# Token-major copies in an RWKV-7 mixer: tensor-engine transposes in place of products with the identity

## The chip, the cores and the metric

The kernel runs on one core of a Trainium2 chip. The metric is the device time of one execution in microseconds, the median of several runs. The engines are TensorE (PE for its matmuls, PEld for its weight loads), VectorE (DVE), ScalarE (ACT), GpSimd (POOL) and SyncE (SP). SyncE, ScalarE and GpSimd also issue DMA transfers.

## The reference

A decoder trunk of two layers runs one step for a prompt (1 sequence of 256 tokens) and a group of samples (8 sequences of 8 tokens), all in float32, with width 1024. Each layer is half a SwiGLU FFN, a token mixer, and half a SwiGLU FFN, each with RMSNorm and a shift, scale and gate that come from a conditioning vector ("ada" below). Layer 0 mixes with a Griffin recurrent block, layer 1 with RWKV-7. The change lies in RWKV-7, which runs this recurrence for 16 heads of 64:

```python
def wkv_scan(r, w, k, v, a, b, S0):
    def step(S, inp):
        r_t, w_t, k_t, v_t, a_t, b_t = inp
        sa = jnp.einsum('bhvk,bhk->bhv', S, a_t)
        S = S * w_t[:, :, None, :] + sa[..., None] * b_t[:, :, None, :] + v_t[..., None] * k_t[:, :, None, :]
        return S, jnp.einsum('bhvk,bhk->bhv', S, r_t)
```

The outputs are the new activations and all recurrent states.

## The kernel before

Prompt and samples are laid side by side as T = 320 columns (256 prompt tokens, then 64 sample tokens). Activations are kept feature-major: a tile is 128 partitions of features by tokens, and there are NT = 8 such tiles, each with two heads. Weights are streamed from HBM by `Weights`: SyncE loads a block of 512 KB into one of five `raw` buffers, and for the large products ScalarE (line 80) and VectorE (line 82) split it into a high and a low part in float32r. `mm3` (lines 174 to 176) then multiplies with three matmuls per block: high by high, high by low, low by high. The conditioning rows come from `Ada` (`ada_ps`, line 190); its `finish` turns them feature-major with transposes of the tensor engine (`ada_tr`, line 206).

RWKV-7 is computed in chunks of 64 tokens: four of the prompt and one of the samples (C5 = 5). A chunk needs copies of some operands with tokens on the partitions. The kernel makes them on TensorE: the feature-major data is the stationary operand, the 128 by 128 identity `eye` streams past it, and the result in PSUM is copied to SBUF. Three places do so:

- `prep(i)`, once per tile: `zw` and `za` (decay and rate), norms `pn` (line 869), `pb` (line 875), the chunk products `g` (line 885), which `mask` turns into the small triangular matrices in `MP` (prompt) and `MS` (samples), and at its end `dt` (line 904): for each of the 5 chunks a 128 by 128 transposed copy of `kk`, evicted by ScalarE into `Dt` (line 905). The bank is PSUM bank 6 for both pieces (chunks 0 to 3, then chunk 4).
- `v_tok(i)`, once per tile: `vt` (line 1078), the values of each chunk in token-major form. The 64 tokens of a chunk go to partitions 64 to 127 of the output, and ScalarE evicts them into the lower half of `UV` (line 1079). Chunks 0 to 3 use bank 2, chunk 4 bank 6.
- `x0t(p)`, four times: `xt` (line 1037), eight 64 by 32 blocks of the inverse `X` each, evicted into `X0T` by ScalarE, and in the call p = 0 by ScalarE and VectorE (lines 1039 and 1040). All are in bank 2.

Between them lies a triangular solve. `prep` sends its small matrices to DRAM (`Mp`, `Ms`) and `invert_s` and `invert_p` load the diagonal blocks back. VectorE inverts the 8 by 8 blocks of the samples and, in 31 steps `s` (lines 976 and 978), the 32 by 32 blocks of the prompt. While it does, TensorE projects the values (`vproj_all`, step V), makes `vt` (step T), multiplies `pw` in `w0` (step O, line 1116; its output is on partitions 0 to 63), and works on the last ada block (step A). Then follow `xt` (step X), the write of `X` to DRAM and the copies of its blocks back into `MP` and `XD` (step D, lines 1046 to 1056), the two products `z` and `x01` of `double` (step Z, lines 1092 and 1101), the samples (`smp`, steps a0 to a7, lines 1133 to 1175), and the chunk recurrence (steps C).

The order of all that is a list written out by hand, `MID`, in which each name takes the next step of its thread:

```python
p7 p7 I V V V V I V V s s s s s s s s V T s s s s s s s s s s A A T s T s s T s T A T A O O s s A s s O A O A
T A s s T s O X X O O A a0 s s X a1 a0 a0 a1 O A A D a0 a0 a2 a2 a2 a1 a2 a1 a1 a2 X Z L Z Q C C C C C C C G0
```

It is the order in which the program is written; the framework then schedules each engine's instructions by their dependencies and priorities (the ada steps have high priority), so the order on an engine can differ from it.

Of the kernel before, what the change touches and what calls it, by code (L numbers as in the profile page):

```python
# [19 lines left out]
T = TP + NB * TS  # L20
# [100 lines left out]
def trunk_kernel(ctx: ExitStack, tc: tile.TileContext, I: dict, O: dict):  # L121
    nc = tc.nc
# [10 lines left out]
    X = [big.tile([128, NT, T], F32, tag="x", name="x")]  # L133
# [5 lines left out]
    eye = const.tile([128, 128], F32, name="eye")  # L139
# [9 lines left out]
    def bank(n, shape, name):  # L149
        return psum.tile(shape, F32, tag=f"p{n}", name=name)  # L150
# [519 lines left out]
    def rwkv_items(nxt):  # L670
# [3 lines left out]
        R = {}  # L674
# [135 lines left out]
        def prep(w, i):  # L810
# [22 lines left out]
            kk = tp.tile([128, C5, 2, 64], F32, tag="kk", bufs=1, name="kk")  # L833
# [15 lines left out]
            t = tp.tile([128, T], F32, tag="xm", bufs=4, name="tk")  # L849
# [10 lines left out]
            for h in range(2):  # L860
                s = slice(64 * h, 64 * h + 64)
# [38 lines left out]
            for n, (c0, c1) in enumerate(((0, 4), (4, 5))):  # L900
                yield
                dt = bank(6, [128, 4, 128], "dt")
                for c in range(c0, c1):
                    nc.tensor.matmul(dt[:, c - c0], kk[:, c].rearrange("p e t -> p (e t)"), eye, start=True, stop=True)
                nc.scalar.copy(out=Dt[:, c0:c1], in_=dt[:, 0:c1 - c0])

        def k_outer(w, i):
# [52 lines left out]
        for i in range(NT):  # L960
            step("R", lambda w, i=i: proj_rk(w, 0, i), [(I["rkv"][0, i], True, 1024)])
            step("v", lambda w, i=i: part_v(w, i))
            steps(f"p{i}", 8, lambda w, i=i: prep(w, i), [(I["w2a2"][i], False, 128)])
# [66 lines left out]
        def x0t(w, p):  # L1030

            if p == 3:
                R["X0T"] = big.tile([32, 64, 32], F32, tag="x", name="X0T")
            X = R["solve"][1]
            ps = bank(2, [32, 8, 64], "xt")
            for s in range(8):
                nc.tensor.matmul(ps[:, s], X[0:64, 8 * p + s], eye[0:64, 0:64], start=True, stop=True)
            o = R["X0T"][:, :, 8 * p:8 * p + 8].rearrange("t m s -> t s m")
            nc.scalar.copy(out=o[:, 0:4], in_=ps[:, 0:4])
            (nc.scalar.copy if p else nc.vector.tensor_copy)(out=o[:, 4:8], in_=ps[:, 4:8])  # L1040
# [28 lines left out]
        def v_tok(w, i):  # L1069
            if i == 0:  # L1070
                R["UV"] = [big.tile([128, 4, C5, 2, 64], F32, tag=n, name="UV") for n in ("xh", "xl")]
            vv = R["v"][:, i]
            nc.gpsimd.memset(R["UV"][i // 4][0:64, i % 4], 0.0)
            uv = R["UV"][i // 4][64:128, i % 4]
            for n, (c0, c1) in enumerate(((0, 4), (4, 5))):
                vt = bank((2, 6)[n], [128, 4, 128], "vt")
                for c in range(c0, c1):
                    nc.tensor.matmul(vt[64:128, c - c0], vv[:, c * 64:c * 64 + 64], eye, start=True, stop=True)
                nc.scalar.copy(out=uv[:, c0:c1].rearrange("p c h v -> p c (h v)"), in_=vt[64:128, 0:c1 - c0])
            nc.vector.tensor_tensor(out=R["bv"][:, i], in0=R["bv"][:, i], in1=vv, op=ALU.mult)  # L1080

        for i in range(NT):
            step("V", lambda w, i=i: vproj_all(w, i), [(I["rkv"][2, i], True, 1024)])
            step("T", lambda w, i=i: v_tok(w, i))
# [96 lines left out]
        for p in (3, 2, 1, 0):  # L1181
            step("X", lambda w, p=p: x0t(w, p))
# [405 lines left out]
```

## Time and profile before

| | |
|---|---|
| median of 3 runs | 1481.87 us (1481.76 to 1485.55) |
| profiled execution | 1483.55 us |
| its span, first to last instruction | 1481.7 us |
| mean granted TensorE clock | 0.987 |
| TensorE busy | 1434.0 us, 97% |
| VectorE, ScalarE, GpSimd busy | 865.1, 670.8, 63.7 us |
| DMA traffic | 266.58 MB, mean 180 GB/s |

All times in views of the profile are counted from the first instruction. A matmul's recorded duration includes its way through the array, so consecutive matmuls overlap in the record, and the distance between their starts is what each costs when they follow each other. The page's chain of work follows the end of the program back from releaser to releaser. In rows by line, "x" is the number of instructions.

### The profile page before, as it was taken

Reading aid. Unit: us, or ns where it says so; the run is one execution under the profiler, and the core shown is the slowest. Engines: PE = TensorE matmul, PEld = TensorE weight load, DVE = VectorE, ACT = ScalarE, POOL = GpSimd, SP = SyncE. Lnnn points to the kernel's source line nnn. Section 1 sums busy time; section 2 is a strip of 40 time slices with the busy share of each in tenths; the row PEclk is TensorE's granted clock in tenths of the full one; section 3 lists DMA queues with packets and bytes.
Section 4 is the critical chain, followed back from the end, with each engine's and each line's share of the span. In section 5 each row is a group of like instructions: output and inputs, shape, how many; then the busy total and the mean of one; then the engine's idle time right before and its main releaser. Section 6 shows DMA issues by size and latency. Waiting matters only on the chain.

```text
span 1481.7 us, 25886 instructions
## 1 busy us (share of the span) xinstructions
PE 1434.0 (97%) x10436; PEld 1307.8 (88%) x10436; DVE 865.1 (58%) x1674; ACT 670.8 (45%) x1215; POOL 63.7 (4%) x170
## 2 busy tenths in 40 slices
PE   5999999999999999999999999999998999999997
PEld 1999999989889999998999998688956779999997
DVE  6644445598874445557444446787754589444444
ACT  4433333488553333445333434386536446343431
POOL 0000000031000000000000003000022100000000
PEclk9999999999999999999999999999999999999998
DMA  8785745457366674546645555223564143444442
GB/s 344 297 302 214 279 139 154 153 207 274 135 238 245 227 269 134 151 149 229 231 176 213 177 152 171 98 70 94 153 218 140 64 154 128 155 157 143 145 148 70
DMA packets 92537, 266.58 MB, mean 180 GB/s; under 512 B 25024, under 2 KB 27456, under 8 KB 91904
## 3 DMA queue, kind: packets, MB, share of 16 engines
q1 hardware_dynamic: 83344, 256.31, 49.9%
q10 hardware_dynamic: 8976, 8.35, 1.8%
q8 instruction: 82, 1.34, 0.4%
q0 software_dynamic: 96, 0.26, 0.1%
q14 instruction: 39, 0.32, 0.1%
HBM read 257.86 MB, written 7.03 MB: 179 GB/s over the span
## 4 chain that ended last, share of the span: by engine, by line
PE 90%; DVE 5%; ACT 2%; DMA 1%; issue 1%; POOL 0%; DVEq 0%; ACTq 0%; POOLq 0%
PE po L176 8%; PE po L174 8%; PE po L175 8%; PE pu L174 7%; PE pg L174 7%; PE pg L176 7%; PE pg L175 7%; PE pu L175 7%; PE pu L176 7%; PE ada_ps L190 5%; PE g L885 1%; PE ps_p L176 1%; PE ps_p L174 1%; PE ps_p L175 1%; DVE lo L82 1%; PE ps_l L769 1%
## 5 line engine op out<-in xcount | busy, mean ns | idle before, releaser
L80 ACT CAST hi<-raw 128x1024 fp32r<-128x1024 f32 (+1 forms) x333 | 340.7, 1023 | 600.7 <-issue 247.9
L82 DVE TENSOR_TENSOR lo<-raw,hi 128x1024 fp32r<-128x1024 f32 (+1 forms) x333 | 396.4, 1191 | 324.9 <-ACT hi L80 324.0
L174 PE MATMUL po<-hh,hi 128*128 128x320 f32 x704 | 217.5, 309 | 0.0
L175 PE MATMUL po<-hl,hi 128*128 128x320 f32 x704 | 217.5, 309 | 0.0
L176 PE MATMUL po<-hh,lo 128*128 128x320 f32 x704 | 217.5, 309 | 0.0
L174 PE MATMUL pu<-mh,hi 128*128 128x320 f32 x608 | 189.9, 312 | 1.5 <-ACT hi L80 1.5
L174 PE MATMUL pg<-mh,hi 128*128 128x320 f32 x608 | 188.5, 310 | 0.0
L176 PE MATMUL pg<-mh,lo 128*128 128x320 f32 x608 | 187.9, 309 | 0.0
L176 PE MATMUL pu<-mh,lo 128*128 128x320 f32 x608 | 187.8, 309 | 0.0
L175 PE MATMUL pg<-ml,hi 128*128 128x320 f32 x608 | 187.8, 309 | 0.0
L175 PE MATMUL pu<-ml,hi 128*128 128x320 f32 x608 | 187.8, 309 | 0.0
L174 PEld LDWEIGHTS po<-hh,hi 128*128 128x128 f32 x704 | 132.1, 188 | 0.0
L175 PEld LDWEIGHTS po<-hl,hi 128*128 128x128 f32 x704 | 132.1, 188 | 0.0
L176 PEld LDWEIGHTS po<-hh,lo 128*128 128x128 f32 x704 | 132.1, 188 | 0.0
L174 PEld LDWEIGHTS pu<-mh,hi 128*128 128x128 f32 x608 | 114.1, 188 | 12.9 <-ACT g L425 10.9
L174 PEld LDWEIGHTS pg<-mh,hi 128*128 128x128 f32 x608 | 114.1, 188 | 5.0 <-ACT hh L418 3.4
L175 PEld LDWEIGHTS pu<-ml,hi 128*128 128x128 f32 x608 | 114.2, 188 | 0.0
L176 PEld LDWEIGHTS pg<-mh,lo 128*128 128x128 f32 x608 | 114.1, 188 | 0.0
L176 PEld LDWEIGHTS pu<-mh,lo 128*128 128x128 f32 x608 | 114.1, 188 | 0.0
L175 PEld LDWEIGHTS pg<-ml,hi 128*128 128x128 f32 x608 | 114.1, 188 | 0.0
L431 DVE TENSOR_TENSOR u<-pu,g 128x320 f32<-128x320 f32 x76 | 37.4, 492 | 127.8 <-PE pu L176 127.8
L190 PE MATMUL ada_ps<-ada_w,sct 128*32 128x512 f32 x448 | 55.0, 610 | 0.0
(383 smaller groups left out, 2405.0 us busy)
## 6 DMA issues: line engine op xcount, KB each, us to landing
raw<-in_ffn_in SPq DMA_DIRECT2D x176, 512.0 KB, 3.2
ada_w<-in_ada_w SPq DMA_DIRECT2D x28, 2048.0 KB, 8.5
raw<-in_ffn_out SPq DMA_DIRECT2D x64, 512.0 KB, 3.5
raw<-in_ada_w SPq DMA_DIRECT2D x32, 512.0 KB, 5.0
raw<-in_ffn_out SPq DMA_DIRECT2D x32, 384.0 KB, 3.1
raw<-in_rkv SPq DMA_DIRECT2D x18, 512.0 KB, 3.2
raw<-in_lru_in SPq DMA_DIRECT2D x16, 512.0 KB, 3.7
raw<-in_lru_out SPq DMA_DIRECT2D x8, 512.0 KB, 3.2
```

Of the source, the lines that this page charges most:

```text
L80: self.nc.scalar.copy(out=hi[:, :n], in_=raw[:, :n])
L82: self.nc.vector.tensor_tensor(out=lo[:, :n], in0=raw[:, :n], in1=hi.bitcast(F32)[:, :n], op=ALU.subtract)
L174: nc.tensor.matmul(ps[:, :n], a, xh[:, k0 + k, :n], start=st, stop=False)
L175: nc.tensor.matmul(ps[:, :n], a, xl[:, k0 + k, :n], start=False, stop=False)
L176: nc.tensor.matmul(ps[:, :n], b, xh[:, k0 + k, :n], start=False, stop=sp)
L190: mm = nc.tensor.matmul(self.ps[r:r + 32, :], sct[:, k, :], wh[:, q * 512:q * 512 + 512], start=(k == 0), stop=(k == NT - 1))
L431: nc.vector.tensor_tensor(out=u, in0=pu[:, :T], in1=st[key, "g"], op=ALU.mult)
L769: nc.tensor.matmul(o[:, :T], lw[:, c0:c1], t, **kw)
L885: nc.tensor.matmul(g[:, c - c0, h], Dp[:, c, h].rearrange("p e t -> p (e t)"), AR[:, c].rearrange("p e t -> p (e t)"), start=True, stop=True)
```

## The change

The three places call `nc.tensor.transpose` instead of `nc.tensor.matmul` with `eye`. For `dt` and `xt` the operands and outputs stay as they are. For `vt` the block that is transposed becomes the 128 tokens that end with the chunk (64 before it and its own 64), taken from the values of all tiles laid end to end (`vf`), so that the output fills all 128 partitions; the upper 64 are read as before. The first block of the first tile has no tokens before it and stays a product.

```diff
@@ prep
                 dt = bank(6, [128, 4, 128], "dt")
                 for c in range(c0, c1):
-                    nc.tensor.matmul(dt[:, c - c0], kk[:, c].rearrange("p e t -> p (e t)"), eye, start=True, stop=True)
+                    nc.tensor.transpose(dt[:, c - c0], kk[:, c].rearrange("p e t -> p (e t)"), eye)
                 nc.scalar.copy(out=Dt[:, c0:c1], in_=dt[:, 0:c1 - c0])
@@ x0t
             for s in range(8):
-                nc.tensor.matmul(ps[:, s], X[0:64, 8 * p + s], eye[0:64, 0:64], start=True, stop=True)
+                nc.tensor.transpose(ps[:, s], X[0:64, 8 * p + s], eye[0:64, 0:64])
@@ v_tok
+            vf = R["v"].rearrange("p i t -> p (i t)")
             vv = R["v"][:, i]
...
                 for c in range(c0, c1):
-                    nc.tensor.matmul(vt[64:128, c - c0], vv[:, c * 64:c * 64 + 64], eye, start=True, stop=True)
+                    e = i * T + c * 64 + 64
+                    if e >= 128:
+
+                        nc.tensor.transpose(vt[:, c - c0], vf[:, e - 128:e], eye)
+                    else:
+                        nc.tensor.matmul(vt[64:128, c - c0], vf[:, e - 64:e], eye, start=True, stop=True)
                 nc.scalar.copy(out=uv[:, c0:c1].rearrange("p c h v -> p c (h v)"), in_=vt[64:128, 0:c1 - c0])
```

## Prediction

> **What bounds the kernel now.** I began with the page's busy shares and its 40 slices, then its chain of work that ended last.
>
> ```profile
> span 1481.7 us, 25886 instructions
> PE 1434.0 (97%) x10436; PEld 1307.8 (88%) x10436; DVE 865.1 (58%) x1674; ACT 670.8 (45%) x1215; POOL 63.7 (4%) x170
> PE   5999999999999999999999999999998999999997
> PE 90%; DVE 5%; ACT 2%; DMA 1%; issue 1%; POOL 0%; DVEq 0%; ACTq 0%; POOLq 0%
> ```
>
> TensorE (PE) is the bound nearly everywhere, but that is an average; the change touches only three places. So next I asked for the three changed lines, and for the one line that already uses a transpose, L206.
>
> ```profile
> L904 PE MATMUL dt<-eye,kk x80: 270/275/377, 989.5 to 1055.5; 128*128 128x128 f32 x80
> L1078 PE MATMUL vt<-eye,v x80: 272/273/324, 1066.2 to 1092.3; 128*64 128x128 f32 x80
> L1037 PE MATMUL xt<-eye,X x64: 216/216/240, 1094.1 to 1105.6; 64*32 64x64 f32 x64
> L206 PE MATMUL ada_tr<-eye,ada_sb x40: 221/273/363, 21.4 to 1109.9; 128*128 128x128 f32 x32, 64*128 64x64 f32 x8
> ```
>
> The counts are the heart of it. The program asks for 40 products at L904 (8 tiles by 5 chunks), 40 at L1078 and 32 at L1037 (4 calls of 8); the trace has 80, 80 and 64 matmuls. Each float32 identity product is issued as two matmuls, each with a weight load. L206 asks for 40 transposes (ten calls of Ada.finish, of 4 each) and the trace has 40: a transpose is one instruction, with the same operands in the same roles (data loaded, identity streamed). All three places lie between 989 and 1106 us. The stages there, by engine:
>
> ```profile
> 1000.00:1020.00 20.00, 20.00 (x139) 17.66 (x139) 14.36 (x34) 13.93 (x30) 1.01 (x8) 1.00 0.29 84
> 1020.00:1040.00 20.00, 19.99 (x148) 17.52 (x147) 16.86 (x41) 13.19 (x31) 1.35 (x10) 1.00 0.35 115
> 1084.00:1093.00 9.00, 9.00 (x112) 5.95 (x104) 8.21 (x24) 3.97 (x11) 1.57 (x4) 1.00 0.78 284
> 1093.00:1105.00 12.00, 11.84 (x113) 6.19 (x111) 1.31 (x6) 4.70 (x11) 1.54 (x3) 1.00 0.76 242
> 1105.00:1114.00 9.00, 6.06 (x168) 3.17 (x170) 2.08 (x8) 0.96 (x2) 0.00 (x0) 0.95 0.95 291
> ```
>
> The columns are the stretch, its length, then PE, PEld, DVE, ACT and POOL busy, the granted clock, DMA share and GB/s. PE is full up to 1105, and after that the DMA engines are. The waits of PE from 1060 to 1115:
>
> ```profile
> PE z L1092 <- issue: 2.5, 1, 2.5
> PE vt L1078 <- ACT UV L1079: 1.7, 3, 1.2
> ```
>
> **The change part by part.** A matmul's duration includes its drain, so what counts is how far apart the matmuls start. These rows of the timeline give start, length and count of runs of equal instructions; (length minus one duration) over (count minus one) is the spacing.
>
> ```profile
> 989.46 0.94 PE L904 MATMUL dt<-eye,kk 128*128 128x128 f32 x7
> 1109.67 0.38 PE L206 MATMUL ada_tr<-eye,ada_sb 128*128 128x128 f32 x2
> 1094.07 0.85 PE L1037 MATMUL xt<-eye,X 64*32 64x64 f32 x12
> 21.41 0.46 PE L206 MATMUL ada_tr<-eye,ada_sb 64*128 64x64 f32 x4 [0.80 <-DVE ada_sb L199]
> 1087.61 1.15 PE L1116 MATMUL pw<-UV,MP 128*64 128x64 f32 x16
> ```
>
> Spacings: identity product of 128 columns (0.94 - 0.275) / 6 = 0.111 us an instruction, 0.222 us a product; transpose of the same shape 0.38 - 0.27 = 0.11 us; xt (0.85 - 0.22) / 11 = 0.057, so 0.114 a product; transpose that streams 64 columns (0.46 - 0.22) / 3 = 0.08 with its slow first one; and (1.15 - 0.22) / 15 = 0.062 for pw, which matters below.
>
> Keys, Dt (L904). 40 products become 40 transposes: 40 x (0.222 - 0.11) = 4.5 us. PE has no idle time in that stage (20.00 and 19.99 of 20), so I count it all. Its cover is thin: VectorE is busy 16.86 of 20 us in the fuller stretch. With PE 4.5 us shorter over about 68 us, VectorE's share rises from 0.84 to about 0.90, still below one. Bounds: 0 (VectorE or ScalarE sets the pace) and 4.5. I take 4.5, as the row has PE at its full length. ScalarE's evictions (L905) stay as they are.
>
> Values, vt (L1078). 39 of 40 products become transposes; the first one (tokens 0 to 63) stays. The data loaded widens from 64 to 128 columns, and the output from 64 to all 128 partitions; only the upper 64 are read. The first call has PE to itself: 4 products at 0.11 less, 0.4 us. The other seven share PE with pw (L1116, the products of w0), and there the trace shows something that the change removes:
>
> ```profile
> 1081.03 0.27 PE L1116 MATMUL pw<-UV,MP 128*64 128x64 f32 x1
> 1081.14 0.27 PE L1078 MATMUL vt<-eye,v 128*64 128x128 f32 x1
> 1081.14 0.22 PE L1116 MATMUL pw<-UV,MP 128*64 128x64 f32 x1
> 1081.25 0.27 PE L1078 MATMUL vt<-eye,v 128*64 128x128 f32 x1
> ```
>
> A pw starts within 0.01 us of a vt and the next vt comes after its usual 0.11: vt writes the upper half of the partitions, pw the lower, and they run side by side, so that pw is free there. A transpose that fills all 128 columns leaves no half. So vt and pw have to be taken together:
>
> ```profile
> 1077.00:1093.00 16.00, 9.14 (x70) 7.45 (x70) 1.00 0.52 178
> 1077.00:1093.00 16.00, 7.78 (x100) 6.71 (x100) 1.00 0.52 178
> 1083.60 0.99 PE ada_ps L190 x8
> 1085.84 1.84 PE ada_ps L190 x12
> 1090.22 0.98 PE ada_ps L190 x4
> ```
>
> The first row is vt alone, the second pw alone; the other three are all the ada work of that stretch, in the chain of work. 16.0 us less 3.8 us of ada and 0.5 us of the waits on UV leaves 11.7 us for 70 vt and 100 pw. Afterwards, with nothing side by side: 35 x 0.11 + 100 x 0.062 = 10.0 us. Saved 1.7 us, where halving alone would have said 3.8; these are the two bounds but for the waits on UV. Those go on: bank 2 must be evicted (L1079) before the next vt writes it, and PE gets there sooner. They are filled by the pw that no longer fit elsewhere, so I charge nothing more; without that filler they cost about 0.25 us for each of seven calls.
>
> The Trainium skill, "TensorEngine Tiling (Array Packing)", Restrictions and Gotchas, says that column tiling and transpose mode of float32 exclude each other. That agrees with the full-width form chosen for vt, and by it the xt transposes below, of 32 columns, would save nothing.
>
> Solve operands, xt (L1037). 32 products of 0.114 us become 32 transposes. The exact form (64 rows, 32 columns loaded) is not in the trace as a transpose. Nearest is the 64-column stream above: 0.08 at most, 0.057 if it is just half of a product. Bounds: 0 (still two passes' time) to 32 x 0.057 = 1.8 us. I take 0.065, nearer to 0.057 because the 0.08 holds a slow first one, hence 32 x 0.05 = 1.6 us. Is PE the bound there? The solve on VectorE, which feeds xt, ends well before its last call:
>
> ```profile
> 1094.29 0.19 DVE L978 TENSOR_TENSOR X<-X,tm 128x31 f32<-128x31 f32 x1
> ```
>
> The last xt starts at 1105.6, 11 us later, and the solve itself hangs on products of the Dt stage, so it moves forward with them. PE can gain 3.7 us on it without meeting it.
>
> What is late next: z (L1092) waits 2.5 us at 1111, for the copy of the diagonal blocks back into MP.
>
> ```profile
> raw<-in_wkv SPq DMA_DIRECT2D x4, 512.0 KB, 5.2
> MP<-xd_d ACTq DMA_DIRECT2D x2, 128.0 KB, 5.8
> ```
>
> ScalarE issues these copies behind its evictions of xt and pa, and SyncE issues the weight loads when PE drops a block, so both move with PE; only the bytes have to pass in less time. Between 1084 and 1105 the DMA engines are busy for 0.77 of the 21 us, which leaves 4.8 us free, against the 3.7 us that PE gains beyond Dt. I take no loss; the bound is all 3.7 us.
>
> Sum: 4.5 + 0.4 + 1.7 + 1.6 = 8.2 us. The profiled execution took 1483.55 us (span 1481.7 and 1.85 around it), so 1475.3 by its own time; it is 1.7 us above the median of the three runs, 1481.87, from which I forecast 1473.7 us. About 0.3% (4.4 us) is what a measurement can tell from no change.
>
> **The rivals.** (a) The wall of DMA at 1105 to 1114: z gets its blocks no earlier relative to the Dt stage, and what vt's later calls and xt saved turns into more waiting there. For it: DMA share 0.95, landings of over 5 us. Against: the free 4.8 us. It keeps 4.5 + 0.4: 1477.0 us.
>
> (b) In the Dt stage VectorE or ScalarE sets the pace, and PE only idles more. For it: 16.86 of 20. Against: PE has no gap there at all. It keeps 3.7: 1478.2 us.
>
> (c) The change does less than it says: the narrow xt form costs as much as two matmuls. 1475.3 us.
>
> (d) The clock, on the other side. After the 2.5 us of idling, the granted clock halves:
>
> ```profile
> 1111.00:1114.00 3.00, 0.54 (x18) 0.38 (x22) 0.04 (x1) 0.37 (x1) 0.00 (x0) 0.84 0.99 303
> 1114.00:1117.00 3.00, 2.99 (x27) 2.20 (x28) 0.69 (x1) 0.83 (x3) 0.20 (x1) 0.50 0.27 53
> 1117.00:1120.00 3.00, 2.80 (x34) 2.61 (x38) 0.00 (x0) 2.08 (x9) 1.12 (x2) 0.52 0.82 250
> ```
>
> At half clock that is (0.16 + 0.50 + 0.48) x 3 / 0.5 = 6.8 us, and it costs PE half of that, 3.4 us a spell. If short transposes and waits on UV let the clock drop in the vt stage, the 27 us from 1066 to 1093 hold four spells, 13.6 us: 1473.7 + 13.6 = 1487.3 us. It decides from the third spell on (10.2 against 8.2). Against it: PE's idle time there is 1.7 us in all, and the clock stood at 1.00. The Trainium skill, "TensorE: Matmul & The Clock Gate", Part 4, says that transposes do not count as activity for the clock gate; no row here has enough of them in a run to show it.
>
> (e) The other way: the stall at 1111 goes with a shifted order of work, and its spell with it: 2.5 + 3.4 us more, 1467.8 us.
>
> **How the numbers follow.** The sum as it stands 0.50, its own range 1471 to 1476; (a) 0.17, (b) 0.12, (c) 0.06, (d) 0.07, (e) 0.08. The forecast is the sum's, 1473.7. The range goes down to (e), 1468, and up past (b) to 1480, for part losses of (a) and (b) together. Faster by over 0.3% means under 1477.4: the sum, (c), (e) and some of (a): 0.69. Within 0.3%: the rest of (a), (b), partial spells: 0.23. Slower: mostly (d), 0.08.
>
> **What would show it.** Counts of 40 at L904, 41 at L1078 (39 transposes and one product of two), 32 at L1037. Spacing of 0.11 for dt and vt; 0.06 to 0.08 for xt, 0.114 if (c). PE still without gaps from 989 to 1056, and the first vt at about 1061.8 instead of 1066.2; if it stays at 1066, (b). No pw starting beside a vt. The last xt near 1098; z's wait near 2.5, or near 6 if (a). A granted clock below 1.00 between 1060 and 1090 would be (d). The prediction is wrong if the order of PE's work comes out so differently that the ada loads or the solve become what PE waits for.

## The result, and the profile after

The change takes the median from 1481.82 us (1480.3 to 1485.55) to 1469.64 us (1468.65 to 1471.03): ratio 0.9908, 95% interval 0.9894 to 0.9922, 12.2 us. (The ratio, here and below, is worked out from all executions; it is not the quotient of the two medians, which is 0.9918 here.) The forecast was 1473.7, so the sign and the range (1468 to 1480) held, and 4 us more came than the sum of its terms. The profiled execution took 1469.47 us.

The page after, its span and busy shares:

```profile
span 1467.6 us, 25663 instructions
PE 1420.6 (97%) x10325; PEld 1294.4 (88%) x10325; DVE 863.2 (59%) x1674; ACT 670.7 (46%) x1215; POOL 63.9 (4%) x170
```

The changed lines after, as the view by line gives them (count, shortest/median/longest ns, first and last start, form). From here on lines behind 1078 stand 6 higher in the changed kernel: L1079 is L1085, w0's L1116 is L1122, z's L1092 is L1098.

```profile
L904 PE MATMUL dt<-eye,kk x40: 270/272/330, 987.9 to 1051.6; 128*128 128x128 f32 x40
L1037 PE MATMUL xt<-eye,X x32: 216/216/229, 1091.2 to 1100.8; 64*32 64x64 f32 x32
L1082 PE MATMUL vt<-eye,v x39: 272/273/476, 1057.0 to 1088.9; 128*128 128x128 f32 x39
L1084 PE MATMUL vt<-eye,v x2: 273/298/323, 1061.7 to 1061.8; 128*64 128x128 f32 x2
```

40, 41 and 32 instructions: one per transpose, as counted. Where the time went is read best from one stretch that holds everything the change touches: from the first chunk product `g` (979.27 us before, 977.72 after) to the first `po` (1203.43 and 1190.14). It is 224.2 us long before and 212.4 after, both in one profiled execution. (The span fell by 14.1 us. Of that 1.6 lie ahead of the first g, where runs differ by themselves: the kernel before with nothing but a later transfer, below, has its first g at 978.10.) The stages up to the last xt and behind it (the columns are those of the prediction: stretch, length, then PE, PEld, DVE, ACT and POOL busy, granted clock, DMA share and GB/s), before:

```profile
980.00:1105.64 125.64, 123.81 (x987) 104.37 (x986) 93.49 (x230) 72.15 (x155) 13.39 (x46) 1.00 0.46 137
1105.64:1203.43 97.79, 88.33 (x1306) 65.24 (x1303) 53.19 (x92) 49.68 (x150) 14.65 (x22) 0.94 0.39 130
```

and after:

```profile
980.00:1100.81 120.81, 117.68 (x864) 95.90 (x863) 91.64 (x229) 70.47 (x151) 13.05 (x46) 0.99 0.47 144
1100.81:1190.14 89.33, 81.48 (x1307) 61.08 (x1304) 51.63 (x92) 50.23 (x151) 15.20 (x23) 1.00 0.41 134
```

The changed matmuls all lie in the first stage, yet that stage, counted from each kernel's first g, became 3.3 us shorter and the second 8.5 us, with as many matmuls in it (1306 and 1307) and the clock at 1.00 instead of 0.94. The clock is the first half of the story. Before, two spells at half clock lie in the second stage (the second runs on to 1205.2, behind the stretch):

```profile
1113.00:1119.85 6.85, 6.00 (x62) 4.96 (x65) 0.69 (x1) 2.76 (x11) 1.17 (x3) 0.50 0.60 160
1198.40:1203.43 5.03, 3.75 (x12) 2.55 (x11) 4.09 (x9) 1.07 (x3) 0.00 (x0) 0.50 0.69 227
```

After, one short one is left in the whole stretch, in the vt stage:

```profile
1073.40:1076.80 3.40, 3.40 (x21) 2.62 (x20) 3.19 (x8) 1.01 (x3) 1.74 (x4) 0.50 0.34 77
```

At a granted clock of 0.50, half of TensorE's busy time in a spell is lost: (6.00 + 3.75) / 2 = 4.9 us before, 1.7 after, a gain of 3.2 us. One execution of each says little about spells that come and go, but the mean granted clocks of all executions agree: 0.992 to 0.995 in the four executions of the change; 0.986 to 0.993 in the 78 of the kernel before that ran beside the experiments, 50 of them at 0.990 or 0.991. A difference of 0.003 over 1470 us is about 4.4 us, as an estimate for a TensorE that is always busy. Both old spells stood behind waits of TensorE: the one of z on its data, which the prediction shows (2.5 us), and this one:

```profile
PE pr L1270 <- DVE gnr L1266: 2.1, 1, 2.1
```

In the waits of TensorE after, z has no wait worth a row, and pr waits 0.35 us. The longest there are these. What x01 (line 1107) waited for the profile does not show; the last of its loads had landed 4 us earlier, at 1115.3.

```profile
PE vt L1082 <- ACT UV L1085: 1.9, 1, 1.9
PE x L1107 <- issue: 1.5, 1, 1.5
PE ps_p L176 <- DVE lo L82: 1.2, 1, 1.2
```

The place of z in the timeline after, with the rows of other products left out:

```profile
1103.45 1.08 PE L1145 MATMUL pa<-raw,ars 128*32 128x128 f32 x32
1106.63 0.39 PE L1098 MATMUL z<-X0T,MP 32*32 32x32 f32 x24
1108.73 0.87 PE L1098 MATMUL z<-X0T,MP 32*32 32x32 f32 x78
1112.10 0.33 PE L1098 MATMUL z<-X0T,MP 32*32 32x32 f32 x16
```

The framework's scheduler put the samples' products (pa) ahead of z and between its parts, so that TensorE works while the blocks for z are on their way.

For every kernel below the same stretch is split in the same way, from the start and end of each matmul record. A matmul is charged from its start to the next start, or to its own end if that comes first; what is left between is idle; half of what lies in a spell at half clock is charged to the clock; the rest is work. A spell that still runs at the first po is cut off there, so the last column follows the clock on to the start of the 61st po, about 10 us further. Against the kernel before (idle 11.5 us, clock 4.9 us, to the 61st po 5.8 us), in us:

| kernel | ratio (95%) | stretch | idle | clock | work | clock to 61st po |
|---|---|---|---|---|---|---|
| the whole change | 0.9908 (0.9894 to 0.9922) | -11.8 | -0.4 | -3.2 | -8.2 | -4.1 |
| Dt alone | 0.9987 (0.9978 to 0.9996) | -1.5 | +3.1 | -0.1 | -4.5 | -0.2 |
| vt alone | 0.9970 (0.9959 to 0.9981) | -4.9 | -1.1 | -4.2 | +0.3 | -2.6 |
| xt alone | 0.9983 (0.9974 to 0.9992) | -3.0 | +2.2 | -2.3 | -2.9 | -1.0 |
| before, z later | 0.9984 (0.9975 to 0.9993) | -3.4 | +2.1 | -3.2 | -2.3 | -2.4 |
| Dt, late reload | 0.9963 (0.9951 to 0.9975) | -5.0 | -1.3 | +0.2 | -3.9 | +0.9 |
| xt, late reload | 0.9947 (0.9934 to 0.9960) | -7.1 | -1.8 | -3.3 | -2.1 | -2.5 |
| before, late reload | 0.9981 (0.9972 to 0.9991) | -4.2 | -1.6 | -3.2 | +0.6 | -4.1 |
| whole, late reload | 0.9915 (0.9903 to 0.9928) | -12.8 | -1.9 | -3.2 | -7.7 | -0.9 |
| Dt and xt | 0.9969 (0.9957 to 0.9981) | -3.7 | +3.1 | -0.4 | -6.3 | +1.2 |
| Dt and xt, late reload | 0.9922 (0.9910 to 0.9934) | -11.7 | -1.9 | -4.9 | -4.9 | -5.8 |
| before, vt widened | 1.0015 (1.0007 to 1.0024) | +1.8 | +1.4 | -3.2 | +3.6 | -2.3 |
| Dt and xt, z later | 0.9942 (0.9927 to 0.9957) | -8.2 | +2.7 | -3.2 | -7.7 | -0.9 |

Each row but its ratio is one profiled execution, and changes outside the touched lines (how matmuls of other tiles happen to overlap) move the work too, by 2.3 us where z alone was moved and no product was touched. Differences of 2 us between rows therefore carry no weight. The work of the whole change is the 8.2 us of the forecast. But by tile it is dt -4.9, xt -2.2, vt with pw -0.3, and -0.8 from the rest, where the value products `ps_p` cost 1.3 more, and pa and ada_ps 1.1 and 0.8 less.

### The profile page after: what moved, and what is told of

It is laid out like the page before. It is cut to its first block, busy times and chain, and to the rows that moved or that the text cites. A ratio compares the mean times of both kernels' runs of the same rounds, so it can differ in the third digit from the quotient of the medians.

```text
span 1467.6 us, 25663 instructions
## 1 busy us (share of the span) xinstructions
PE 1420.6 (97%) x10325; PEld 1294.4 (88%) x10325; DVE 863.2 (59%) x1674; ACT 670.7 (46%) x1215; POOL 63.9 (4%) x170
## 4 chain that ended last, share of the span: by engine, by line
PE 89%; DVE 6%; ACT 2%; DMA 1%; issue 1%; POOL 0%; ACTq 0%; DVEq 0%; SPq 0%; POOLq 0%
PE po L176 8%; PE po L174 8%; PE po L175 8%; PE pu L174 7%; PE pg L174 7%; PE pg L176 7%; PE pg L175 7%; PE pu L175 7%; PE pu L176 7%; PE ada_ps L190 4%; PE g L885 1%; DVE lo L82 1%; PE ps_p L176 1%; PE ps_p L174 1%; PE ps_l L769 1%; PE ps_p L175 1%
## 5 line engine op out<-in xcount | busy, mean ns | idle before, releaser
L82 DVE TENSOR_TENSOR lo<-raw,hi 128x1024 fp32r<-128x1024 f32 (+1 forms) x333 | 396.5, 1191 | 323.8 <-ACT hi L80 322.9
```

Source lines behind the costliest of these rows:

```text
L82: self.nc.vector.tensor_tensor(out=lo[:, :n], in0=raw[:, :n], in1=hi.bitcast(F32)[:, :n], op=ALU.subtract)
```

## The experiments

**One part at a time.** Each of the three edits of the diff was made by itself in the kernel before.

Dt alone (L904 only):

> Only the key copies (Dt) are transposes; vt and xt stay products. Theory 1 (the gain is TensorE time, which goes through to the end): 40 products at 0.11 us less, 4.5 us, so about 1477.3 where before is 1481.8. Theory 2 (most of the 12.2 us comes from the order of work that the scheduler makes anew, and from its stalls and half-clock spells): the part can come out anywhere between -10 and +3 us, and the three parts do not add up to the whole. The wait of z at about 1111 us and the half clock behind it stay under theory 1.

Measured: 1481.67 us against 1482.97, ratio 0.9987. The work fell by 4.5 us as it should, and the idle time grew by 3.1 us, with one long wait behind the solve:

```profile
PE x L1101 <- DMA XD<-xd_d: 5.1, 1, 5.1
```

x01 (line 1101) reads `XD`, which four loads bring back from DRAM (line 1052). The last x01 matmul starts at 1127.28, where it was before (1127.37): all that Dt saved was gone by then.

vt alone (L1078 and the lines around it):

> Only the value copies (vt) are transposes. Theory 1: 0.4 us of the first call and 1.7 us of the others, 2.1 us, so about 1479.7; pw no longer starts beside a vt. Theory 2: it is off from that by more than 2 us either way. If the loss of the second half of the array costs as much as the halved vt saves (what the trace of the changed kernel hints at: vt and pw together take as long as before), 1481 to 1482.

Measured: 1480.16 us, ratio 0.9970. Its ratio is lower than that of Dt alone, and lower than that of xt alone by less than the intervals can tell. The gain is not one of work: vt and pw together cost 0.2 us more than before. z ended 4.5 us later than in the kernel before, and nothing waited for `XD`.

xt alone (L1037 only):

> Only the solve operands (xt) are transposes. Theory 1: 32 products at 0.05 us less, 1.6 us, about 1480.2, with a spacing of 0.056 us in the xt rows. Theory 2: off by more than 2 us either way, as z and the samples behind it are ordered anew.

Measured: 1481.12 us, ratio 0.9983. xt went from 4.37 to 2.20 us, and x01 then waited 5.5 us for `XD`. The last x01 came 0.9 us earlier, where the last xt had come 4.7 us earlier. The three ratios together make 0.0060, the whole change 0.0092, so the parts don't add up.

z later, the kernel before with nothing else changed:

```diff
+            with tc.issue_after(R["py", 1]):        # z behind sample tile 1's py
                 for j in range(16):
```

> The kernel before with all its products; only z (the first product of the doubling) is queued on TensorE behind the sample products of tiles 0 and 1 (their py), which is where the changed kernel has it. Theory 2: the 2.5 us wait at z has work in it, and the half clock that follows goes too: 3 to 6 us faster, 1476 to 1479, without a single transpose. Theory 1 (order is a bystander): within 1 us of before, since z itself comes no earlier and the chain behind it sets the end.

Measured: 1480.99 us, ratio 0.9984: a gain from order alone, with every product with the identity in place, but less than the 3 to 6 us that were expected of it. The last x01 came 4.9 us earlier, though z started later.

These four point at the loads of `XD`, and at what moves beside them. `reload` (step L, line 1108) brings the 1.3 MB of x back for the residual at the mixer's end. It writes the buffer tagged "x", which `X0T` occupies until z has read it, so it is issued as soon as z ends. The view by line of the `XD` loads and of the reload: instructions, lengths of the issue in ns, first and last issue, and the time from issue to landing (shortest/median/longest). In the kernel before:

```profile
L1052 SPq DMA_DIRECT2D XD<-xd_d x4: 326/480/486, 1115.5 to 1116.9; - x4
DMA to landing us min/median/max: 2.0/4.6/7.1
L1108 ACTq DMA_DIRECT2D x<-x_dram x1: 344/344/344, 1116.5 to 1116.5; - x1
```

With Dt alone:

```profile
L1052 SPq DMA_DIRECT2D XD<-xd_d x4: 325/481/984, 1112.7 to 1114.1; - x4
DMA to landing us min/median/max: 5.3/5.6/5.7
L1108 ACTq DMA_DIRECT2D x<-x_dram x1: 345/345/345, 1110.0 to 1110.0; - x1
```

In the whole change:

```profile
L1052 SPq DMA_DIRECT2D XD<-xd_d x4: 325/480/487, 1110.6 to 1112.0; - x4
DMA to landing us min/median/max: 1.9/2.4/3.3
L1114 ACTq DMA_DIRECT2D x<-x_dram x1: 371/371/371, 1112.5 to 1112.5; - x1
```

Where the reload goes out first (Dt alone, and xt alone with it at 1108.1 us against 1113.6), the loads of 64 KB are slow and x01 waits for them (with Dt alone the first of them lands after 5.5 us instead of 2.0, so by estimate 3.5 of the 5.1 us are the reload's); in the kernel before it goes out among them, and the slowest takes 7.1 us; where it goes out behind them (the whole change, and vt alone and z later as well), x01's wait on them is gone. A saving that brings z forward brings the reload forward, and the reload then takes the DMA engines from the very loads that are next on the path.

**The reload moved, and nothing else.** The next four kernels test that. The edit:

```diff
-                (nc.sync if q % 2 else nc.sync).dma_start(out=R["XD"][0]...)
+                R["xd_ld"] = nc.sync.dma_start(out=R["XD"][0]...).ins
...
-            nc.scalar.dma_start(out=X[0], in_=R["xd"])
+            with tc.issue_after(R["xd_ld"]): nc.sync.dma_start(out=X[0], in_=R["xd"])
```

> The Dt transposes alone, and the 1.3 MB reload of x that ScalarE's queue issued as soon as z had read its buffer now issued by SP's queue behind the four XD loads. Theory W (the saved PE time is lost because an earlier z starts the reload earlier, and the reload then runs beside the XD loads that x01 waits for): the XD loads land within 6 us of xd_d's landing instead of 7.2, the wait of x01 on XD falls from 5.1 us to under 3, the last x01 matmul comes 2.5 to 4 us before that of the kernel before instead of 0.1, and the time is about 1478.7 (ratio 0.9960 to 0.9980 where the Dt transposes alone had 0.9987). Theory O (what counts is which work the scheduler left in PE's queue beside the wait; the reload costs the XD loads nothing): the last x01 matmul stays within 0.5 us of the kernel before, ratio 0.9978 to 0.9996.

> The xt transposes alone, with the reload of x behind the XD loads as well. W: the wait of x01 on XD falls from 5.5 us to under 3, the last x01 matmul comes 2.5 to 4 us before that of the kernel before instead of 0.9, time about 1478.5 (ratio 0.9955 to 0.9978 where the xt transposes alone had 0.9983). O: the last x01 matmul stays within 0.5 us of where the xt transposes alone had it, ratio 0.9974 to 0.9992.

> The kernel before with nothing but the reload of x moved behind the XD loads: no transpose in it. W: in the kernel before two of the four XD loads ran beside the reload and landed 5 us behind the other two, so these come 3 to 4 us earlier, the last x01 matmul 2 to 4 us earlier, and the time is 1479 to 1481 (ratio 0.997 to 0.999). O: nothing before the end of the solve changes, the last x01 matmul moves by less than 1 us, ratio 0.999 to 1.001.

> The whole change with the reload of x moved behind the XD loads. W: its reload was issued behind the XD loads already (1112.5 against 1110.6 to 1112.0 us), so the end of the solve stays within 0.5 us and the time within 1.5 us of the whole change's (ratio 0.990 to 0.992); a small gain is possible because MP's last load, which ran beside the reload, lands earlier. O: the same. A loss of over 2 us would say that the reload on SP's queue has a price of its own, and that the other three kernels of this set read too slow by it.

Measured: Dt 1477.13, xt 1475.56, before 1479.90, whole 1470.74 us, against 1482.89; the ratios are in the table. The reload went out at 1117 to 1127 us in all four, and in the kernel before with it the loads landed in 1.9 to 3.1 us:

```profile
L1052 SPq DMA_DIRECT2D XD<-xd_d x4: 326/480/487, 1114.5 to 1116.0; - x4
DMA to landing us min/median/max: 1.9/2.3/3.1
L1108 SPq DMA_DIRECT2D x<-x_dram x1: 406/406/406, 1127.1 to 1127.1; - x1
```

The wait of x01 on `XD`, 5.1 and 5.5 us, is gone in both. Times of Dt, before and whole lie in W's ranges, and xt gained still more than its range; theory O as it was written is out, as it had Dt at 0.9978 or above. That the reload slows the loads is shown by their landing times. One number of W missed: the last x01 came 0.9 us (Dt), 2.4 us (xt) and not at all (before) earlier, not 2 to 4 us. The scheduler put samples' products ahead of x01, which then finished no sooner but with that work done; the gain shows at the first po instead (6.3, 8.0 and 5.4 us earlier than before). And since the later order changes with the edit, part of what these kernels gain is a wait gone further on: pr, which waited 2.1 us before, waits 0.4 us in all four. Its spell did not go with the wait: around the first po three of the four still have one, of 3.4, 3.4 and 6.8 us (Dt, xt, whole). How much of what these kernels gain (3.0 us in the third) is the collision and how much that order, these runs don't separate.

Set against the kernel before with a late reload, the whole change with one is 0.9915 / 0.9981 = 0.9934, 9.8 us (about 2.4 us either way from the two intervals), which is near the sum of 8.2.

**Is vt worth anything?** Dt and xt without vt, with the reload where it was and with the late one:

> Dt and xt by transposes, vt by identity products as before; the reload of x where it was. The reload theory: with 5.2 us less of Dt and 2.4 us less of xt on TensorE z ends still earlier, and unless other work stands ahead of z in TensorE's queue the reload is issued before the XD loads, which then land 7 us or more behind xd_d: x01 waits 4 us or more on XD and the time is 1476 to 1480 (ratio 0.9955 to 0.998). If the reload falls behind the XD loads, as it did in the whole change, about 1471 to 1474. A sum of the two parts alone, with no wall, would be 1482.9 - 1.9 - 2.5 = 1478.5, so a time below 1475 says that the wall, not the work, held the single parts back.

> Dt and xt by transposes, vt by identity products, and the reload of x behind the XD loads: against the whole change with the same reload it leaves out the vt transposes alone. If the vt transposes cost more than they save (TensorE's time for vt and pw together was 16.4 us with them and 15.8 us without), this is as fast or faster than the whole change with the late reload: 1469 to 1471.5 (ratio 0.990 to 0.9925), and vt and pw together take 15.8 to 16.2 us. If they are worth the 2.1 us of the forecast, this is slower by that much: 1472 to 1474 (ratio 0.9925 to 0.994).

Measured: 1479.21 us (0.9969) and 1471.78 us (0.9922) against 1483.21. Without vt the change runs into the wall: the reload goes out at 1107.7 us, the loads at 1112.7, and

```profile
PE x L1101 <- DMA XD<-xd_d: 5.8, 1, 5.8
PE pr L1270 <- DVE gnr L1266: 2.1, 1, 2.1
```

6.3 us of work saved, 3.1 us of it idled away, and the old wait of pr and its spell still there. With the late reload the same two edits come to 0.9922, which can't be told from the whole change with it (0.9915, the intervals overlap). So the vt transposes are worth the 9 us between 0.9969 and 0.9908 where the reload collides, and nothing that shows where it doesn't: vt and pw hardly save work, and the order changes with them. On what the second of these kernels was to decide, its time stands between the two forecasts (1469 to 1471.5 and 1472 to 1474) and its ratio in the first (0.990 to 0.9925), at the edge of the second.

**Why vt saves no work.** The products were widened to 128 columns without becoming transposes:

```diff
-                    nc.tensor.matmul(vt[64:128, c - c0], vv[:, c * 64:c * 64 + 64], eye, start=True, stop=True)
+                    e = i * T + c * 64 + 64
+                    if e >= 128:
+                        nc.tensor.matmul(vt[:, c - c0], vf[:, e - 128:e], eye, start=True, stop=True)
+                    else:
+                        nc.tensor.matmul(vt[64:128, c - c0], vf[:, e - 64:e], eye, start=True, stop=True)
```

> The kernel before with the vt identity products widened from 64 to 128 columns of stationary operand and no transpose: the number of TensorE instructions of vt and their moving columns are as before, only the part of the array that they fill is doubled. If vt and pw ran side by side in the two halves of the array before, that ends: vt and pw together take 18.5 to 20.5 us of TensorE instead of 15.8, no pw runs between two vt at once, and z ends 3 to 4.5 us later. If what vt costs is its own instructions alone, the two together stay within 0.5 us of 15.8. The time follows less surely, 1482 to 1487 (ratio 0.9995 to 1.003), because a later z also puts the reload of x behind the XD loads, which was worth 3.0 us.

Measured: 1485.44 us, ratio 1.0015 (1.0007 to 1.0024). The time in which TensorE has a vt or a pw in the array rose from 15.8 to 20.7 us (18.5 to 20.5 were expected), with the same count of instructions. z ended 8.2 us later, more than the 4.9 us and than the 3 to 4.5 expected, as the order changed as well; the time stayed in its range because the reload then fell behind the loads. In the timeline of the widened kernel vt and pw follow each other in runs, and no pw starts beside a vt:

```profile
1079.16 0.68 PE L1122 MATMUL pw<-UV,MP 128*64 128x64 f32 x8
1079.77 1.38 PE L1082 MATMUL vt<-eye,v 128*128 128x128 f32 x10
1081.08 0.68 PE L1122 MATMUL pw<-UV,MP 128*64 128x64 f32 x8
```

Before, 34 of the 128 pw start within 0.03 us of a vt, and here none. The widening also lengthens vt's weight loads, from 137 to 192 ns, but that is not what costs: inside a run of ten the vt are 0.123 us apart and were 0.115, 0.6 us over 80. So the side-by-side running in the halves of the array is shown. Losing it cost 4.9 us, those 0.6 included, and the transposes win back 4.2 of that: with vt alone the two take 16.5 us.

**The order without vt.** Last, Dt and xt with z queued behind the samples' second tile, by the same edit as above and the reload on ScalarE's queue:

> Dt and xt by transposes, vt by identity products, the reload of x on ScalarE's queue as in the kernel before, and z queued on TensorE behind the second sample tile's step (py of tile 1), which is about where the whole change's order had it. If what the vt transposes brought to the whole change is only that order, this version has it without them: z ends behind 1110 us, the reload is issued behind the XD loads, no wait of x01 on XD over 2 us is left (5.8 us where Dt and xt stood alone), and the time is 1470 to 1473 (ratio 0.991 to 0.993). If the vt transposes bring something of their own, the time stays above 1474 (ratio over 0.9938) with the wait gone.

Measured: 1475.43 us, ratio 0.9942. The reload went out behind the `XD` loads and x01's long wait went, as expected, but the time stayed above 1474. By what was written ahead, that would speak for something of vt's own. The table doesn't bear that out as work (-7.7 us, against -8.2 of the whole change) or as clock in the stretch (-3.2 in both). The difference in the stretch is idle time, 3.1 us, in waits that the order set by hand brings:

```profile
PE po L1360 <- ACT zh L1331: 2.5, 1, 2.5
PE pa L1140 <- DMA raw<-in_wkv: 1.1, 1, 1.1
PE x L1102 <- DVE XD L1096: 1.0, 1, 1.0
```

po waits 1.1 us in the whole change; the 2.5 us stand where z alone was moved, too. Behind them, past the end of the stretch, comes a spell at half clock, which costs another 3 us:

```profile
1193.60:1200.40 6.80, 6.22 (x22) 5.82 (x23) 5.40 (x12) 1.54 (x4) 0.00 (x0) 0.50 0.30 123
```

That the whole order of the change, put into a kernel without vt, would give its time stays unshown. A narrow vt transpose, 64 columns into partitions 64 to 127, was not tried. No version beat the change beyond its interval.

## Why the prediction was right or wrong

**Dt.** Forecast 4.5 us, measured 4.9 (9.35 to 4.49 us of work in dt). TensorE is still full to the end of that stage (64.0 of the 64 us from 988 to 1052), so rival (b), VectorE setting the pace there, is out. Right behind the stage a small part of it came, which the prediction had at nothing: every kernel with these transposes waits 0.5 to 1.2 us for VectorE's split (`ps_p` on L82, at 1064 to 1067) and no kernel without them does. In the same kernels `ps_p` also takes 1.3 to 1.5 us more work, so that some 2 to 2.5 us of what Dt saves goes again right behind it.

**xt.** Forecast 1.6, measured 2.2. The timeline of the whole change has four such rows, one for each call:

```profile
1092.97 0.62 PE L1037 MATMUL xt<-eye,X 64*32 64x64 f32 x8
```

(0.62 - 0.216) / 7 = 0.058 us a transpose, as if just half of a product; I had taken 0.065. That dt and xt came out above the prediction's own upper bounds, 4.5 and 1.8, has one reason: these were spacings inside a run. Charged to the next start, a product cost 0.234 us for dt and 0.137 for xt, not 0.222 and 0.114, and a transpose 0.112 and 0.069. Rival (c) is out, and so is the prediction's reading of the Trainium skill, "TensorEngine Tiling (Array Packing)", Restrictions and Gotchas, by which they would save nothing: these transposes of 32 columns cost half of the products. Whether the array was tiled for them no row shows, so what the page states, that column tiling and the transpose mode of float32 exclude each other, is neither borne out nor refuted.

**vt.** Forecast 2.1, measured 0.3 in the whole change and -0.2 (a loss) alone. This step failed. Its first half, that the transposes end the side-by-side running, was right. What was mis-sized is the 10.0 us afterwards, 35 x 0.11 + 100 x 0.062: spacings inside a run, with nothing for the change from one run to the next. The timeline after shows what a change costs:

```profile
1077.44 0.77 PE L1082 MATMUL vt<-eye,v 128*128 128x128 f32 x5
1078.13 0.80 PE L1122 MATMUL pw<-UV,MP 128*64 128x64 f32 x10
1078.86 0.77 PE L1082 MATMUL vt<-eye,v 128*128 128x128 f32 x5
```

Five transposes take 0.69 us to the next start, 0.138 each, and ten pw 0.73 us, 0.073 each. At those prices the same 35 and 100 cost 12.1 us, more than the 11.7 that I had for before.

**The clock in the vt stage.** Rival (d) happened once: the wait on UV grew to 1.9 us and a 3.4 us spell followed it, 1.7 us lost, far from the three spells where (d) decides. This wait, the spell and the work that vt did not save are also why the last xt came at 1100.8 and not near 1098. With Dt and xt alone, where vt is still a product, the same spell stands at the same place, in the view of stretches,

```profile
1073.90:1077.30 3.40, 3.40 (x30) 3.24 (x29) 3.19 (x8) 0.74 (x2) 1.11 (x2) 0.50 0.34 77
```

behind a wait of 2.0 us:

```profile
PE vt L1078 <- ACT UV L1079: 2.3, 2, 2.0
```

So the spell is not owed to the vt transposes. Nor does a wait of that length always bring one: with Dt alone, vt waited 1.9 us and no spell followed. The Trainium skill, "TensorE: Matmul & The Clock Gate", Part 4, says that transposes don't count as activity for the clock gate; nothing in these runs needs that.

**What is late next.** I had reckoned in bytes, 4.8 us of free DMA time against 3.7 us, and named z. For the whole change that came out, by luck of order. As reasoning it failed: for Dt alone, xt alone and the two together the wall was real (rival (a), 5.1, 5.5 and 5.8 us), at x01 and not at z, and it was set in the main by which of two transfers went first. I had not looked for what z's end releases: the reload. The bytes counted as well: the write of `X` to DRAM that the `XD` loads wait for (line 1046, SyncE's queue) took 7.6 us to land in the whole change and 6.2 before, and had landed before the reload went out. There TensorE had the samples' products to do meanwhile.

**The 4 us beyond.** They are for the most part the clock of rival (e), to which I gave 0.08: the stall at z and its spell went with a shifted order, and so did the wait of pr and, in this execution, its spell. Work -8.2, clock -3.2 and idle -0.4 make 11.8 us of the stretch. The idle time fell by little because other waits came: x01's 1.5 us, `ps_p`'s 1.2, and 1.1 at the first po. That the sum of terms was right in total (8.2 us) is luck, with its parts wrong both ways: dt and xt 1.0 us too small, vt 1.8 too large, and 0.8 from the rest, which I had not.

## What to carry to other kernels

Where work ahead of a hand-over is shortened, list what each instruction at the end of that work releases, buffers too: a large transfer that isn't urgent but whose buffer comes free sooner can start in front of the small one that is next on the path. Try each part of a change alone before crediting it: here the part that saved no work was worth 9 us beside the other two, while the order moved with it, and one edit on a DMA queue gave 7 of the 9 without it. And price short runs of matmuls by the distance to the next run's start, not by the spacing inside a run.

## What the hardware showed that was not expected

- A matmul that uses 64 columns of the array and one that uses the other 64 ran beside each other; doubling the columns of one of them, with the same count of matmuls of the same length, cost 4.9 us over 80 vt and 128 pw (15.8 to 20.7 us).
- A float32 transpose of 32 columns started every 0.058 us, half of the 0.114 us of the product with the identity.
- In the vt stage a spell at half clock followed waits of 1.8 us (Dt with late reload), 1.9 (the change) and 2.0 (Dt and xt, with z later too), and none followed waits of 1.2 (before) and 1.6 (the change with late reload, and Dt and xt with it). But none followed the 1.9 us of Dt alone either, and around z spells came with no wait of that length (before with late reload, at 1117.4 us). What brings a spell stays open.
